# First convolution's projection from rows transposed before their norm's scale is known

## The chip, the cores and the metric

The kernel runs on one core of a Trainium2 chip. The time is that of one execution on the device in microseconds. In the profile PE is the tensor engine (matmuls), PEld its weight loads, DVE the vector engine, ACT the scalar engine, POOL the GpSimd engine and SP the engine that issues the DMA transfers of weights. PEclk is the tensor engine's granted clock as a share of its full speed (1.00 is 2.4 GHz, 0.50 is 1.2 GHz).

## The reference, cut to what matters

Two transformer layers work on 256 rows of 1024 numbers in float32. The change touches the head of the first one: the root-mean-square norm, the projections of the normed rows, and the short causal convolution over the rows that stands behind three of them.

```python
def rmsnorm(x, g):
    y = x * lax.rsqrt(jnp.mean(x * x, axis=-1, keepdims=True) + EPS)
    return y * g

h = rmsnorm(x, norm1_g)
parts = split_cols(h @ w_in)              # q, k, v (512 each), z, beta, alpha (8 each),
                                          # b_q, b_k, b_v, i_q, i_k, i_w, gates
qkv = silu(causal_dwconv(concat([a_q, a_k, a_v]), conv_w))
...
o_a = gated_delta_rule(aq, ak, av, g, beta)
o_b = dsa_attention(bq, bk, bv, iq, ik, iw)
merged = gate_a * (o_a @ w_proj_a) + gate_b * (o_b @ w_proj_b)
x = x + merged @ w_out
x = x + hier_moe(rmsnorm(x, norm2_g), ...)
```

A second layer (a gated recurrence, attention, a feed-forward block) follows; the change doesn't touch it. The norm multiplies each row by one number, its inverse root. A product of the rows with a weight matrix can therefore take that number in before or behind the product, row by row.

## The kernel before, in words

Every large product runs in split precision. An operand is held as a high part (ACT copies it to a rounded float32 type) and a low part (DVE subtracts the high part from it), and each product of 128 columns of the inner dimension is three matmuls: high x high, high x low, low x high. For weights the two parts are `whi` (L298, ACT) and `wlo` (L301, DVE), made from `raw`, which SP's queue loads 512 KB at a time (`wload`, L306); each of the three has a ring of four buffers. For the activations they are the two halves of `hx`, the tiles of an `HT` object: four tiles, each with two blocks of 128 columns.

The normed rows are needed transposed, with the inner dimension on the partitions. A transpose is a matmul of 128 columns of x by a matrix: by the identity it only transposes, by `dg`, the identity times each row's inverse root (L212, DVE), it scales the rows as well. `square` (L217, ACT) sums the squares of half a row at a time, and `row_scale` finds the inverse root from them in some twelve small steps on DVE, then makes `dg`. In the program before, all 16 blocks (two groups of 128 rows, eight blocks each) are scaled transposes (L492), four to a tile of PSUM. DVE multiplies each four by the norm's gain (L495) into `h`, and pairs of blocks are split from there (L254 on ACT, L255 on DVE) into `hT`. The gain, and the weights of the convolution, come from `arow`, whose 56 rows are transposed once (L482) and copied to `ap`.

`hT` feeds, in this order of the program: `zps`, the narrow product for beta and alpha (L543 to L545, 16 columns); `conv(1)`, which makes k, and `conv(0)`, which makes q. `conv` calls `fm`, which multiplies 128 columns of weights at a time with all 256 rows (L373 to L375) in groups of two sums, and for each of the four sums calls `em`: ACT copies the sum from PSUM into `zc` and, scaled, into `cy`; DVE adds the three earlier rows (three L563); ACT takes the tanh; DVE makes the result (L566). Then comes the chain of the delta rule, a generator that `stream` runs up to its mark "v": it takes the softplus of alpha (L386 and behind), works on q and k for each group of rows (DVE, ACT, PE, and four products on POOL, L652 to L657), inverts small triangular blocks with a long row of small DVE steps, and then joins them with products of 64 x 64 (`prod`, L731). Behind it in the program stand `conv(2)` for v, the rest of the chain, and then the projections for the second mixer in four groups (`z_group`: two of 292 columns into `zI`, two of 384 into `zB`), which run in `tm` (L333 to L335), 192 matmuls in all, and the gates (512 columns).

The order on each engine is fixed ahead of the run: a scheduler takes the program and places each instruction by its own estimates of when operands and buffers are there. So a change at the head moves instructions far behind it. PSUM has three tiles for sums (`acc`) and three for the small products of the first stage (`sm`). SP's queue starts with x's first half, the identity (the first 128 columns of the constants `cst`), the two parts of `arow`, x's second half, and then the rest of the constants (L526, 1 MB) ahead of the first weights.

Of the kernel before, what the change touches and what calls it, by code (L numbers as in the profile page):

```python
# [18 lines left out]
S = 256  # L19
# [52 lines left out]
def body(ctx, tc, I, out, dbg=None):  # L72
# [13 lines left out]
    def nm(s):  # L86
        cnt[0] += 1
        return f"{s}{cnt[0]}"
# [74 lines left out]
    SY.dma_start(xt[0][:, 0:512], I["x"][0, 0:128, 0:512])  # L163
    SY.dma_start(xt[0][:, 512:], I["x"][0, 0:128, 512:])
    SY.dma_start(ident, I["cst"][:, 0:128])
    SY.dma_start(arow[48:56], I["norm1_g"][0].rearrange("(r c) -> r c", c=128))
    SY.dma_start(arow[0:48], I["conv_w"][0].rearrange("j (r c) -> (j r) c", c=128))
    SY.dma_start(xt[1], I["x"][0, 128:256, :])
# [306 lines left out]
    dgs = []  # L475
    for t in range(2):
        q = tiny([128, 2])
        for hf in range(2):
            square(xt[t][:, hf * 512:(hf + 1) * 512], q[:, hf:hf + 1])
        dgs.append(row_scale(q)[1])  # L480
# [4 lines left out]
    n1 = ap[:, 48:56]  # L485
    hT = HT(8)
    h32 = [b4([128, 4, S], n="h32") for _ in range(2)]
    for t in range(2):
        for j in range(2):
            ps = sm()  # L490
            for k in range(4):
                T.matmul(ps[:, k * 128:(k + 1) * 128], xt[t][:, (4 * j + k) * 128:(4 * j + k + 1) * 128], dgs[t],  # L492
                         start=True, stop=True)
            y = h32[j][:, :, t * 128:(t + 1) * 128]
            V.tensor_tensor(y, ps.rearrange("p (k t) -> p k t", k=4),  # L495
                            n1[:, 4 * j:4 * j + 4, None].to_broadcast([128, 4, 128]), op=ALU.mult)
            for i in range(2):
                split_psum(y[:, 2 * i:2 * i + 2], *(hT.pair(2 * j + i, q, t * 128, (t + 1) * 128) for q in range(2)))
# [53 lines left out]
    qT, kT, vT = (a4([128, 4, S], n="qkvT") for _ in range(3))  # L552

    def conv(i, dst):
        def em(f, ps):
            zc = sp.tile([128, S + 3], F32, tag="zc", name=nm("zc"), bufs=2)
            G.memset(zc[:, 0:3], 0.0)
            A.activation(zc[:, 3:], ps, AF.Copy)
            y = cv("cy")
            cw = [ap[:, j * 12 + i * 4 + f:j * 12 + i * 4 + f + 1] for j in range(4)]  # L560
            A.activation(y, ps, AF.Copy, scale=cw[3])
            for j in (2, 1, 0):
                V.scalar_tensor_tensor(y, zc[:, j:j + S], cw[j], y, op0=ALU.mult, op1=ALU.add)  # L563
# [1247 lines left out]
```

## Time and profile before

| what | us |
| --- | --- |
| median of three runs | 882.61 |
| lowest and highest of them | 880.13 and 883.9 |
| the profiled execution's own time | 878.45 |
| span of its trace | 876.7 |
| PE busy in the span | 828.0 |
| DVE busy in the span | 599.9 |

The profiled execution is a run of its own, a little faster than the three timed ones. The span runs from the first to the last instruction recorded; the time holds another 1.75 us around it. In the rows further down a matmul's own duration is longer than its pace, since matmuls overlap: the time from one start to the next tells what one costs.

### The profile page before, as it was taken

To read this page: it belongs to the slowest core of one execution; us is meant where nothing else is said; L and a number is where in the kernel's file an instruction comes from. 1 tells how busy PE (TensorE), PEld (TensorE's weight loads), DVE (VectorE), ACT (ScalarE), POOL (GpSimd) and SP (SyncE) were. 2 spreads that over 40 slices of the span, in tenths; PEclk is the share of its full clock that TensorE was granted. 3 is DMA by queue.
4 is the path that set the end of the run, shared out by engine and by line. 5 is a ranking of instruction groups with operands and counts; after the bars stand their busy time and mean duration, and the time that the engine had idled before them with its cause. 6 is when DMAs were issued, how large, how long until landed. Compare 5 with 4: busy or idle time off the path is not lost.

```text
span 876.7 us, 14583 instructions
## 1 busy us (share of the span) xinstructions
PE 828.0 (94%) x5541; PEld 692.7 (79%) x5541; DVE 599.9 (68%) x1301; ACT 418.5 (48%) x742; POOL 59.1 (7%) x74
## 2 busy tenths in 40 slices
PE   5998999999998999998798998999999999999997
PEld 4997878888987665654797985889888888888876
DVE  5977996987677242425769788666886666674564
ACT  5743544566452111114664544665566555663443
POOL 5022030000000000000116002000000000000000
PEclk9999999999998999999899998999999999999999
DMA  8633561345489899965453563255665666665541
GB/s 247 191 87 78 170 194 50 96 148 180 155 324 312 291 397 339 388 202 171 147 149 82 163 208 108 73 170 190 214 197 157 182 190 189 182 211 198 193 157 48
DMA packets 107577, 162.81 MB, mean 186 GB/s; under 512 B 7256, under 2 KB 73312, under 8 KB 107504
## 3 DMA queue, kind: packets, MB, share of 16 engines
q1 hardware_dynamic: 106864, 161.71, 57.9%
q8 instruction: 45, 0.74, 0.3%
q0 software_dynamic: 640, 0.13, 0.2%
q14 instruction: 28, 0.23, 0.1%
HBM read 159.71 MB, written 2.11 MB: 185 GB/s over the span
## 4 chain that ended last, share of the span: by engine, by line
PE 43%; DVE 6%; issue 2%; ACT 1%; POOL 0%; DVEq 0%; POOLq 0%; ACTq 0%
PE acc L368 13%; PE acc L369 6%; PE acc L335 5%; PE acc L334 5%; PE acc L333 5%; PE acc L374 1%; PE acc L375 1%; PE acc L373 1%; PE sm L272 1%; DVE wlo L301 1%; PE sm L1656 1%; PE sm L1560 1%; PE sm L1684 1%; DVE ST L1561 0%; PE sm L1676 0%
## 5 line engine op out<-in xcount | busy, mean ns | idle before, releaser
L301 DVE TENSOR_TENSOR wlo<-raw,whi 128x1024 fp32r<-128x1024 f32 (+4 forms) x203 | 240.0, 1185 | 93.4 <-ACT whi L298 91.6
L298 ACT ACTIVATE whi<-raw 128x1024 fp32r<-128x1024 f32 (+4 forms) x203 | 207.0, 1022 | 147.8 <-PE acc L335 53.4
L368 PE MATMUL acc<-hx,whi 128*128 128x512 f32 x608 | 212.0, 400 | 0.9 <-DVE hx L255 0.9
L369 PE MATMUL acc<-hx,wlo 128*128 128x256 f32 x608 | 160.6, 284 | 0.0
L333 PE MATMUL acc<-whi,hx 128*128 128x512 f32 (+3 forms) x368 | 138.5, 376 | 6.8 <-ACT zI L814 3.7
L334 PE MATMUL acc<-wlo,hx 128*128 128x512 f32 (+3 forms) x368 | 137.2, 373 | 0.1
L335 PE MATMUL acc<-whi,hx 128*128 128x512 f32 (+3 forms) x368 | 137.3, 373 | 0.0
L368 PEld LDWEIGHTS acc<-hx,whi 128*128 128x128 f32 x608 | 109.4, 188 | 22.4 <-DVE hx L255 1.1
L369 PEld LDWEIGHTS acc<-hx,wlo 128*128 128x128 f32 x608 | 114.6, 189 | 8.2 <-issue 1.0
L333 PEld LDWEIGHTS acc<-whi,hx 128*128 128x128 f32 x368 | 69.8, 190 | 18.0 <-ACT zI L814 4.5
L374 PE MATMUL acc<-hx,whi 128*128 128x256 f32 x288 | 82.4, 286 | 1.4 <-DVE hx L258 1.4
L373 PE MATMUL acc<-hx,whi 128*128 128x256 f32 x288 | 81.6, 286 | 1.5 <-ACT hx L257 1.5
L375 PE MATMUL acc<-hx,wlo 128*128 128x256 f32 x288 | 82.7, 288 | 0.0
L335 PEld LDWEIGHTS acc<-whi,hx 128*128 128x128 f32 x368 | 69.8, 190 | 10.0 <-issue 0.2
L334 PEld LDWEIGHTS acc<-wlo,hx 128*128 128x128 f32 x368 | 69.9, 190 | 9.3 <-DVE wlo L301 0.4
L1247 PE MATMUL acc<-we,xg 128*64 128x256 f32 x512 | 64.8, 383 | 0.0
L374 PEld LDWEIGHTS acc<-hx,whi 128*128 128x128 f32 x288 | 55.9, 194 | 2.0 <-DVE hx L258 1.8
L373 PEld LDWEIGHTS acc<-hx,whi 128*128 128x128 f32 x288 | 55.5, 194 | 2.4 <-ACT hx L257 2.0
L375 PEld LDWEIGHTS acc<-hx,wlo 128*128 128x128 f32 x288 | 56.0, 195 | 0.4 <-issue 0.2
L1247 PEld LDWEIGHTS acc<-we,xg 128*64 128x64 f32 x512 | 37.8, 137 | 21.3 <-issue 5.4
L379 ACT ACTIVATE both<-acc 128x256 f32<-128x256 f32 x76 | 28.8, 380 | 33.4 <-PE acc L368 33.4
L380 DVE TENSOR_TENSOR both<-both,acc 128x256 f32<-128x256 f32 x76 | 31.7, 416 | 16.6 <-ACT both L379 15.7
(456 smaller groups left out, 1119.2 us busy)
## 6 DMA issues: line engine op xcount, KB each, us to landing
raw<-in_w_in SPq DMA_DIRECT2D x64, 512.0 KB, 3.7
we<-in_w_exp_gate SPq DMA_DIRECT2D x32, 512.0 KB, 7.6
we<-in_w_exp_up SPq DMA_DIRECT2D x32, 512.0 KB, 8.0
wd<-in_w_exp_down SPq DMA_DIRECT2D x64, 256.0 KB, 6.0
raw<-in_w_ffn_gate SPq DMA_DIRECT2D x22, 512.0 KB, 3.8
raw<-in_w_ffn_up SPq DMA_DIRECT2D x22, 512.0 KB, 3.8
raw<-in_w_ffn_down SPq DMA_DIRECT2D x22, 512.0 KB, 4.3
raw<-in_w_out SPq DMA_DIRECT2D x16, 512.0 KB, 4.4
```

Source lines behind the costliest of these rows:

```text
L298: A.activation(hi[:, :n], raw[:, :n], AF.Copy)
L301: (eng or V).tensor_tensor(lo[:, :n], raw[:, :n], hi[:, :n].bitcast(F32), op=ALU.subtract)
L333: T.matmul(ps[t][:, :n], ht.hi(kk, a, b), wh[:, k], start=kk == 0, stop=False)
L334: T.matmul(ps[t][:, :n], ht.hi(kk, a, b), wl[:, k], start=False, stop=False)
L335: T.matmul(ps[t][:, :n], ht.lo(kk, a, b), wh[:, k], start=False, stop=kk == K - 1)
L368: two = [lambda: T.matmul(ps[f], wh[:, k, c], ht.both(kk), start=kk == 0, stop=kk == K - 1), lambda: T.matmul(ps[f][:, :S], wl[:, k, c], h ...
L369: lambda: T.matmul(ps[f][:, :S], wl[:, k, c], ht.hi(kk), start=False, stop=False)]
L373: T.matmul(ps[f][:, :S], wh[:, k, c], ht.hi(kk), start=kk == 0, stop=False)
L374: T.matmul(ps[f][:, :S], wh[:, k, c], ht.lo(kk), start=False, stop=False)
L375: T.matmul(ps[f][:, :S], wl[:, k, c], ht.hi(kk), start=False, stop=kk == K - 1)
L380: V.tensor_tensor(both, both, ps[f][:, :S], op=ALU.add)
L1247: T.matmul(ph[64 * q:64 * q + 64, i * 256:(i + 1) * 256], xgs[pr // 2][k // 4][:, k % 4, e * 64:(e + 1) * 64], ups[ex][k // 4, i][:, k % 4 ...
```

## The change

x's four quarters now go first on SP's queue, and the identity and `arow` go to ACT's queue. `arow` is transposed first. Then all 16 blocks are transposed by the identity alone (L270), as soon as x is there, and each block is split on its own with the gain as the scale (`transpose_in` with `gk`: L257 on ACT, L258 on DVE, 128 columns each) into a first `HT`, `rT`. The squares stand behind that, with all the steps of the inverse roots. Two matmuls of a matrix of ones with `dg` (L494) spread the inverse roots of all rows over the 128 partitions, and ACT copies them to `rrow`. `conv(1)` runs on `rT`, and its `em` takes each sum from PSUM by a product with `rrow` on DVE (L510) in place of ACT's copy; ACT then makes `cy` from that. Behind `conv(1)` the 16 blocks are made once more, scaled (L272), and split block by block (L257, L258) into `hT`, which `conv(0)` and everything behind it use. `zps` comes after that. The load of the constants' rest now stands behind four weight loads on SP's queue.

```diff
--- before.py
+++ after.py
@@ -160,12 +160,12 @@
 
     xt = [b4([128, D], n="x") for _ in range(2)]
     arow = sp.tile([56, 128], F32, tag="t128", name=nm("arow"), bufs=4)
-    SY.dma_start(xt[0][:, 0:512], I["x"][0, 0:128, 0:512])
-    SY.dma_start(xt[0][:, 512:], I["x"][0, 0:128, 512:])
-    SY.dma_start(ident, I["cst"][:, 0:128])
-    SY.dma_start(arow[48:56], I["norm1_g"][0].rearrange("(r c) -> r c", c=128))
-    SY.dma_start(arow[0:48], I["conv_w"][0].rearrange("j (r c) -> (j r) c", c=128))
-    SY.dma_start(xt[1], I["x"][0, 128:256, :])
+    A.dma_start(ident, I["cst"][:, 0:128])
+    for t in range(2):
+        for hf in range(2):
+            SY.dma_start(xt[t][:, hf * 512:(hf + 1) * 512], I["x"][0, t * 128:(t + 1) * 128, hf * 512:(hf + 1) * 512])
+    A.dma_start(arow[48:56], I["norm1_g"][0].rearrange("(r c) -> r c", c=128))
+    A.dma_start(arow[0:48], I["conv_w"][0].rearrange("j (r c) -> (j r) c", c=128))
 
 
     def rsqrt(v, shape):
@@ -472,30 +472,53 @@
 
 
     w_in = I["w_in"][0]
-    dgs = []
-    for t in range(2):
-        q = tiny([128, 2])
-        for hf in range(2):
-            square(xt[t][:, hf * 512:(hf + 1) * 512], q[:, hf:hf + 1])
-        dgs.append(row_scale(q)[1])
     gps = sm()
     T.transpose(gps[:, 0:56], arow, ident[0:56, 0:56])
     ap = cpool.tile([128, 56], F32, name="ap")
     V.tensor_copy(ap, gps[:, 0:56])
     n1 = ap[:, 48:56]
+
+    rT = HT(8)
+    for j in range(2):
+        for t in range(2):
+            transpose_in({t: xt[t]}, ht=rT, ts=(t,), js=(j,), gk=n1)
+    qs_ = [tiny([128, 2]) for _ in range(2)]
+    for t in range(2):
+        for hf in range(2):
+            square(xt[t][:, hf * 512:(hf + 1) * 512], qs_[t][:, hf:hf + 1])
+    ones_ = sp.tile([128, 128], F32, tag="t128", name=nm("one"), bufs=4)
+    V.memset(ones_, 1.0)
+    dgs = [row_scale(q)[1] for q in qs_]
+    rps = sm()
+    for t in range(2):
+        T.matmul(rps[:, t * 128:(t + 1) * 128], ones_, dgs[t], start=True, stop=True)
+    rrow = b1([128, S], n="rr")
+    A.activation(rrow, rps[:, 0:S], AF.Copy)
+
+    qT, kT, vT = (a4([128, 4, S], n="qkvT") for _ in range(3))
+
+    def conv(i, dst, ht, scale=None):
+        def em(f, ps):
+            zc = sp.tile([128, S + 3], F32, tag="zc", name=nm("zc"), bufs=2)
+            G.memset(zc[:, 0:3], 0.0)
+            y = cv("cy")
+            cw = [ap[:, j * 12 + i * 4 + f:j * 12 + i * 4 + f + 1] for j in range(4)]
+            if scale is None:
+                A.activation(zc[:, 3:], ps, AF.Copy)
+                A.activation(y, ps, AF.Copy, scale=cw[3])
+            else:
+                V.tensor_tensor(zc[:, 3:], ps, scale, op=ALU.mult)
+                A.activation(y, zc[:, 3:], AF.Copy, scale=cw[3])
+            for j in (2, 1, 0):
+                V.scalar_tensor_tensor(y, zc[:, j:j + S], cw[j], y, op0=ALU.mult, op1=ALU.add)
+            th = cv("ct")
+            A.activation(th, y, AF.Tanh, scale=0.5)
+            V.scalar_tensor_tensor(dst[:, f], th, 1.0, y, op0=ALU.add, op1=ALU.mult)
+        fm(ht, w_in, i * 512, 4, em)
+    conv(1, kT, rT, rrow)
     hT = HT(8)
-    h32 = [b4([128, 4, S], n="h32") for _ in range(2)]
     for t in range(2):
-        for j in range(2):
-            ps = sm()
-            for k in range(4):
-                T.matmul(ps[:, k * 128:(k + 1) * 128], xt[t][:, (4 * j + k) * 128:(4 * j + k + 1) * 128], dgs[t],
-                         start=True, stop=True)
-            y = h32[j][:, :, t * 128:(t + 1) * 128]
-            V.tensor_tensor(y, ps.rearrange("p (k t) -> p k t", k=4),
-                            n1[:, 4 * j:4 * j + 4, None].to_broadcast([128, 4, 128]), op=ALU.mult)
-            for i in range(2):
-                split_psum(y[:, 2 * i:2 * i + 2], *(hT.pair(2 * j + i, q, t * 128, (t + 1) * 128) for q in range(2)))
+        transpose_in({t: xt[t]}, ht=hT, dg={t: dgs[t]}, ts=(t,), gk=n1)
 
     prow = cpool.tile([44, 128], F32, name="prow")
     G.dma_start(prow[0:16], I["b_gate"][0].rearrange("(r c) -> r c", c=128))
@@ -549,24 +572,7 @@
         T.transpose(zp2[:, t * 16:(t + 1) * 16], zbT[:, t * 128:(t + 1) * 128], ident[0:16, 0:16])
     V.tensor_copy(zb, zp2[:, 0:32].rearrange("p (t c) -> p t c", t=2))
 
-    qT, kT, vT = (a4([128, 4, S], n="qkvT") for _ in range(3))
-
-    def conv(i, dst):
-        def em(f, ps):
-            zc = sp.tile([128, S + 3], F32, tag="zc", name=nm("zc"), bufs=2)
-            G.memset(zc[:, 0:3], 0.0)
-            A.activation(zc[:, 3:], ps, AF.Copy)
-            y = cv("cy")
-            cw = [ap[:, j * 12 + i * 4 + f:j * 12 + i * 4 + f + 1] for j in range(4)]
-            A.activation(y, ps, AF.Copy, scale=cw[3])
-            for j in (2, 1, 0):
-                V.scalar_tensor_tensor(y, zc[:, j:j + S], cw[j], y, op0=ALU.mult, op1=ALU.add)
-            th = cv("ct")
-            A.activation(th, y, AF.Tanh, scale=0.5)
-            V.scalar_tensor_tensor(dst[:, f], th, 1.0, y, op0=ALU.add, op1=ALU.mult)
-        fm(hT, w_in, i * 512, 4, em)
-    conv(1, kT)
-    conv(0, qT)
+    conv(0, qT, hT)
 
     def hv(ap):
 
@@ -803,7 +809,7 @@
 
     dl_ = delta()
     stream("a", dl_)
-    conv(2, vT)
+    conv(2, vT, hT)
     stream("a", dl_)
 
     zB = [b4([128, 768], n="zB") for _ in range(2)]
```

The order of PE at the head, before: `sm` are PSUM tiles of small products, `x_74` and `x_75` the two groups of rows, `dg` the scales, `hx` the split blocks, `acc` the sums of 128 columns.

```order
L482 MATMUL sm_127<-cst,arow_76 128x56
L492 MATMUL sm_137<-dg_103,x_74 128x128 x4
L492 MATMUL sm_147<-dg_103,x_74 128x128 x4
L492 MATMUL sm_157<-dg_125,x_75 128x128 x4
L492 MATMUL sm_167<-dg_125,x_75 128x128 x4
L528 MATMUL sm_203<-cst,prow 128x44
L543 MATMUL acc_213<-hx_131,whi_216 16x256
L373 MATMUL acc_252<-hx_131,whi_256 128x256
L373 MATMUL acc_253<-hx_131,whi_256 128x256
```

After, the first nine:

```order
L476 MATMUL sm_84<-cst,arow_76 128x56
L270 MATMUL sm_92<-cst,x_74 128x128 x4
L270 MATMUL sm_105<-cst,x_75 128x128 x4
L270 MATMUL sm_118<-cst,x_74 128x128 x4
L270 MATMUL sm_131<-cst,x_75 128x128 x4
L373 MATMUL acc_198<-hx_88,whi_202 128x256
L374 MATMUL acc_198<-hx_88,whi_202 128x256
L373 MATMUL acc_199<-hx_88,whi_202 128x256
L374 MATMUL acc_199<-hx_88,whi_202 128x256
```

The scaled transposes ahead of the first sum (L492) have become unscaled ones (L270); `zps` (L543) is gone from the head, and the first sum is worked on with nothing between. In the order after, the scaled transposes stand behind the whole of `conv(1)` (`acc_283` is `conv(1)`'s last sum, `acc_494` and `acc_495` are `conv(0)`'s first, `acc_458` is `zps`):

```order
L375 MATMUL acc_283<-hx_91,wlo_318 128x256
L272 MATMUL sm_370<-dg_171,x_74 128x128 x4
L272 MATMUL sm_383<-dg_171,x_74 128x128 x4
L272 MATMUL sm_396<-dg_188,x_75 128x128 x4
L566 MATMUL acc_458<-hx_366,whi_461 16x256
L373 MATMUL acc_494<-hx_366,whi_498 128x256
L373 MATMUL acc_495<-hx_366,whi_498 128x256
L567 MATMUL acc_458<-hx_366,whi_461 16x256
L568 MATMUL acc_458<-hx_366,wlo_463 16x256
L374 MATMUL acc_494<-hx_366,whi_498 128x256
```

Three of the four groups stand there in a row; the last (`sm_409`) follows twelve matmuls of `conv(0)` and `zps` later. On DVE in the same place, before, in `conv(1)`'s sums (`cy`, `ct` and `zc` are the tiles of `em`, `qkvT` its result, `t` the softplus):

```order
L301 TENSOR_TENSOR wlo_456<-raw_452,whi_454 128x1024
L566 SCALAR_TENSOR_TENSOR qkvT_250<-ct_322,cy_317 128x256
L563 SCALAR_TENSOR_TENSOR cy_328<-zc_325,ap,cy_328 128x256
L390 TENSOR_SCALAR t_603<-t_601 128x16
L563 SCALAR_TENSOR_TENSOR cy_328<-zc_325,ap,cy_328 128x256
L392 RECIPROCAL t_605<-t_603 128x16
L563 SCALAR_TENSOR_TENSOR cy_328<-zc_325,ap,cy_328 128x256
L301 TENSOR_TENSOR wlo_510<-raw_506,whi_508 128x1024
L566 SCALAR_TENSOR_TENSOR qkvT_250<-ct_333,cy_328 128x256
L563 SCALAR_TENSOR_TENSOR cy_401<-zc_398,ap,cy_401 128x256
```

And after:

```order
L301 TENSOR_TENSOR wlo_584<-raw_580,whi_582 128x1024
L513 SCALAR_TENSOR_TENSOR cy_273<-zc_271,ap,cy_273 128x256
L258 SCALAR_TENSOR_TENSOR hx_366<-sm_370,ap,hx_366 128x128
L510 TENSOR_TENSOR zc_355<-acc_283,rr_193 128x256
L516 SCALAR_TENSOR_TENSOR qkvT_196<-ct_279,cy_273 128x256
L513 SCALAR_TENSOR_TENSOR cy_346<-zc_344,ap,cy_346 128x256
L258 SCALAR_TENSOR_TENSOR hx_366<-sm_370,ap,hx_366 128x128
L513 SCALAR_TENSOR_TENSOR cy_346<-zc_344,ap,cy_346 128x256
L258 SCALAR_TENSOR_TENSOR hx_366<-sm_396,ap,hx_366 128x128
L513 SCALAR_TENSOR_TENSOR cy_346<-zc_344,ap,cy_346 128x256
L258 SCALAR_TENSOR_TENSOR hx_367<-sm_370,ap,hx_367 128x128
```

The softplus steps have gone behind, and the products with `rrow` (`rr_193`, L510) and the second set of splits (L258 into `hx_366` and on) have come in between `conv(1)`'s sums. The third place is PE around the first triangular product of the chain. Before, in the last of the four groups of `z_group` (`acc_1700`; `acc_2190` is the first sum of the gates):

```order
L333 MATMUL acc_1700<-whi_1757,hx_134 128x384
L334 MATMUL acc_1700<-wlo_1759,hx_134 128x384
L335 MATMUL acc_1700<-whi_1757,hx_134 128x384
L333 MATMUL acc_1700<-whi_1757,hx_134 128x384
L731 MATMUL sm_924<-DD_905,LT_632 64x64 x16
L334 MATMUL acc_1700<-wlo_1759,hx_134 128x384
L335 MATMUL acc_1700<-whi_1757,hx_134 128x384
L333 MATMUL acc_2190<-whi_2194,hx_131 128x512
L334 MATMUL acc_2190<-wlo_2196,hx_131 128x512
L335 MATMUL acc_2190<-whi_2194,hx_131 128x512
L731 MATMUL sm_943<-DT_906,X_941 64x64 x16
```

And after, where `acc_1773` and `acc_1774` are the sums of the last group for the two groups of rows:

```order
L335 MATMUL acc_1698<-whi_1755,hx_369 128x384
L333 MATMUL acc_1773<-whi_1777,hx_366 128x384
L334 MATMUL acc_1773<-wlo_1779,hx_366 128x384
L335 MATMUL acc_1773<-whi_1777,hx_366 128x384
L333 MATMUL acc_1773<-whi_1777,hx_366 128x384
L334 MATMUL acc_1773<-wlo_1779,hx_366 128x384
L335 MATMUL acc_1773<-whi_1777,hx_366 128x384
L737 MATMUL sm_998<-DD_979,LT_706 64x64 x16
L333 MATMUL acc_1774<-whi_1777,hx_366 128x384
```

Of the 192 matmuls of the four groups, 190 stand ahead of the first triangular product (L731) before, and 150 ahead of the same product (L737) after; the others follow it. `conv(2)` stands whole ahead of the second row half's products (L665 before, L671 after) in the order after.

## Rows read from the trace of the kernel before

**Rows 1.** The page's first part: busy us, share of the span, instructions.

```profile
PE 828.0 (94%) x5541; PEld 692.7 (79%) x5541; DVE 599.9 (68%) x1301; ACT 418.5 (48%) x742; POOL 59.1 (7%) x74
```

**Rows 2.** Stretches: length; busy of PE, PEld, DVE, ACT, POOL; PEclk; DMA share; GB/s.

```profile
24.00:48.00 24.00, 23.77 (x197) 23.34 (x197) 23.56 (x65) 16.35 (x33) 0.80 (x8) 1.00 0.62 173
48.00:104.00 56.00, 50.46 (x404) 47.04 (x403) 45.70 (x128) 22.54 (x41) 11.77 (x10) 0.97 0.38 113
0.00:104.00 104.00, 87.83 (x692) 82.49 (x693) 84.18 (x237) 51.84 (x100) 24.31 (x44) 0.98 0.55 158
105.90:130.00 24.10, 23.07 (x410) 19.40 (x410) 23.28 (x44) 12.31 (x19) 6.41 (x8) 1.00 0.64 194
130.00:220.00 90.00, 90.00 (x679) 75.27 (x678) 72.84 (x194) 53.51 (x119) 2.56 (x3) 1.00 0.40 120
```

**Rows 3.** Timeline of the start: start, length, engine, instruction, [idle before, what ended it].

```profile
3.50 0.63 ACT L217 ACTIVATE junk<-x 128x512 f32<-128x512 f32 x1 [1.47 <-DMA x<-in_x]
...
4.26 0.63 ACT L217 ACTIVATE junk<-x 128x512 f32<-128x512 f32 x1
...
5.58 0.32 PE L482 MATMUL sm<-cst,arow 56*128 56x56 f32 x1 [5.58 <-DMA arow<-in_conv_w]
...
13.18 1.04 ACT L298 ACTIVATE whi<-raw 128x1024 fp32r<-128x1024 f32 x1
...
13.52 2.05 PE L492 MATMUL sm<-dg,x 128*128 128x128 f32 x16 [1.73 <-DVE hx L255]
...
15.91 0.29 PE L543 MATMUL acc<-hx,whi 128*16 128x256 f32 x1 [0.15 <-ACT hx L254]
```

**Rows 4.** Timeline of PE in a convolution and in a 384-column projection.

```profile
20.93 0.28 PE L374 MATMUL acc<-hx,whi 128*128 128x256 f32 x1
21.05 0.28 PE L375 MATMUL acc<-hx,wlo 128*128 128x256 f32 x1
...
97.46 0.33 PE L333 MATMUL acc<-whi,hx 128*128 128x384 f32 x1
97.64 0.33 PE L334 MATMUL acc<-wlo,hx 128*128 128x384 f32 x1
```

**Rows 5.** Timeline near 424 us, where another norm is split block by block.

```profile
424.59 0.62 ACT L257 ACTIVATE hx<-sm,par 128x128 fp32r<-128x128 f32 x2 [0.42 <-DVE hx L258]
...
424.99 0.61 DVE L258 SCALAR_TENSOR_TENSOR hx<-sm,par,hx 128x128 fp32r<-128x128 f32 x2
```

**Rows 6.** Timeline of DVE at the start and in the convolutions.

```profile
11.83 0.69 DVE L495 TENSOR_TENSOR h<-sm,ap 128x512 f32<-128x512 f32 x1
...
13.03 1.09 DVE L255 TENSOR_TENSOR hx<-h,hx 128x256 fp32r<-128x256 f32 x3
...
29.78 1.22 DVE L301 TENSOR_TENSOR wlo<-raw,whi 128x1024 fp32r<-128x1024 f32 x1
30.91 0.42 DVE L566 SCALAR_TENSOR_TENSOR qkvT<-ct,cy 128x256 f32<-128x256 f32 x1
31.25 0.48 DVE L563 SCALAR_TENSOR_TENSOR cy<-zc,ap,cy 128x256 f32<-128x256 f32 x1
31.64 0.17 DVE L394 TENSOR_TENSOR t<-t,t 128x16 f32<-128x16 f32 x1
```

**Rows 7.** Timeline of the delta chain: GpSimd's second row half, the first triangular product.

```profile
75.00 1.90 POOL L652 TENSOR_TENSOR dl<-t,cst 128x512 f32<-128x512 f32 x1 [11.19 <-DVE t L648]
...
105.91 0.80 PE L731 MATMUL sm<-DD,LT 64*64 64x64 f32 x20
```

**Rows 8.** PE's longest wait behind 48 us, and two stretches with their PEclk.

```profile
85.23 0.44 PE L333 MATMUL acc<-whi,hx 128*128 128x384 f32 x1 [3.24 <-ACT zI L814]
...
86.40:89.60 3.20, 3.20 (x12) 3.20 (x11) 3.06 (x11) 0.00 (x0) 0.00 (x0) 0.50 0.70 157
96.80:101.00 4.20, 4.18 (x24) 4.12 (x24) 4.13 (x13) 0.70 (x1) 0.00 (x0) 1.00 0.98 344
```

## What the change was predicted to do

> **What bounds the kernel now.** I read the page's busy shares first: the tensor engine (PE) has work for 94% of the span, the vector engine (DVE) for 68% [rows 1]. Shares are averages, so next the stretches [rows 2]. From 130 to 220 us PE is busy for all 90 us: whatever it owes when it comes there is paid in full. From 24 to 48 us both engines are full (PE 23.8, DVE 23.6 of 24), so that a longer DVE queue holds up PE. From 48 to 104 us PE works 50.5 and DVE 45.7 of 56: here the chain of the delta rule passes back and forth between DVE, GpSimd and PE. The edit works on the first 48 us, and its price is read in two places: when PE has finished `conv(0)`, and how much independent matmul work is left for PE when the chain's first triangular product (L731, at 105.91 [rows 7]) may run. Behind 220 us the two programs' PE orders are the same again but for small exchanges, so a lead or a lag is handed on.
>
> **The start.** PE's unbroken run begins at 15.91 [rows 3], after the squares, the inverse root, the scaled transposes and their splits. In the changed program the raw transposes need no root. ScalarE (ACT) sets their pace: its first square still begins at 3.50, since x's first half lands as before; L482 and its copy, which give the norm's gain column, come some 0.5 earlier than at 5.58, so the first split can run at about 5.7. Ahead of the first weight copy ACT then has 11 split copies (two take 0.62 [rows 5], so 0.31 each) and three more squares (3.50 to 4.26, so 0.76 each [rows 3]): 3.4 + 2.3 = 5.7, to 11.4; with that copy (1.04 [rows 3]) the first matmul of `conv(1)` stands at 12.5: **3.4 us earlier**. The wait for the first low half of the weights behind it (one L301) I count as in the program before.
>
> **Work added to PE.** The 16 raw transposes lie in time in which PE has nothing to do. The scaled ones don't any more: before, they ran ahead of 15.91; now they stand between `conv(1)` and `conv(0)`, 16 matmuls in two passes each. The second half of them took 2.05 us for 16 passes [rows 3], so **+4.1 us**; the two matmuls that spread the scale are four passes, +0.5.
>
> **Work added to DVE.** Removed: four L495 (0.69 long, about 0.6 of the queue) and eight L255 (three in 1.09, so 0.36) [rows 6]: 2.4 + 2.9 = 5.3. Added: 32 split subtractions of 128 columns (two in 0.61, so about 0.28 in a run [rows 5]) = 9.0, and four products of a PSUM sum with the scale row. No row shows that product; the nearest are L566 (0.34 from one to the next) and L563 (0.39) [rows 6], so 1.4 to 1.6; by the PSUM read of L495 taken at half its width it would be 1.2. Sum: **+5.2 us**, in the stretch in which DVE is full.
>
> **The stall between the convolutions.** PE ends `conv(1)` at 12.5 + 0.75 (first wait) + 96 x 0.12 [rows 4] + 0.5 = 25.3 and the first three groups of scaled transposes at 28.4. Then it needs the second set of splits. They stand in DVE's queue among the work on `conv(1)`'s sums. That queue gets there late: up to the first sum it holds 16 subtractions (4.5), some two dozen steps of the two roots (0.15 each, 3.6), four L301 (1.13 each, 4.5) and the scale diagonals (0.6), 13.2 us from 5.4 on, plus some 1.5 of waiting for ACT, so 20.1 to 20.4. From there to the last split: 4 products 1.4, 12 L563 4.7, 4 L566 1.4, 3 L301 3.4, 16 subtractions 4.6, small ones 0.6: 16.1, and some 0.7 of waiting: 37.3. PE has only the narrow product for beta and alpha, 18 matmuls of `conv(0)` and the last scaled group to fill 28.4 to 37.3: 42 x 0.12 + 1.0 + 0.3 = 6.3. **Stall: 2.6 us**; 0 if DVE had no waits at all and PE came late, 4 if ACT's alternation with DVE costs full turns (0.40 from copy to subtraction in both directions [rows 5]). At the end of `conv(0)` PE therefore lies -3.4 + 4.1 + 0.5 + 2.6 = **+3.8 us** behind.
>
> **The delta chain.** The order shows the second price. Before, 190 of the 192 matmuls of the index and attention projections stand ahead of the first L731; now 150 do. The 40 are 384 columns wide, 0.175 each [rows 4]: **7.0 us** of PE work not yet done when the chain's products start. When is that? DVE was busy 84.2 of the first 104 us [rows 2]. Now +5.2, less the four weight halves that now stand behind it (768 columns each, three quarters of 1.13: -3.4): 86.0. Its idle time before was 19.8. Of this 5.4 at the start remain; I find 4 to 5 of small waits to the end of `conv(0)`, and twice 3 to 4.5 in which it waits for GpSimd's four products (first at 75.00 in the second half row [rows 7]), since the softplus steps no longer lie under the convolution and there is less to fill with: 18.5 in all, so 104.5 where 104 was. L731 then moves by +0.5, and 7.0 + 0.5 less the 1.0 us that PE waits in 105.9 to 130 now (24.1 - 23.1 [rows 2]), which owed work can fill, is **+6.5 us**.
>
> The two counts, +3.8 if nothing further is lost and +6.5 by the order, bound the forecast; I take the middle, **+5.2 us**. The profiled execution took 878.45 us (span 876.70 and 1.75 around it), which becomes 883.7. The runs shown have a median of 882.61, 4.2 above it; on that scale: **887.8 us**. Its own range is 885 to 890.
>
> The DMA edits cost nothing: the identity and the gain rows leave x's queue, and the rest of the constants goes behind four weight tiles; two copies of L1034/L1035 and the narrow weights' copy on ACT then wait for it, ahead of the last split copy. That split is needed by PE at about 18.3, and I put the landing there too; a microsecond later would show as a microsecond of PE wait.
>
> **Rivals.**
> A, DVE's waits go (not slower). DVE has 10.3 us idle from 48 to 104 [rows 2]; if the added 5.2 us fill them and the chain reaches L731 at 100.9, then -5 + 7.0 - 1.0 = +1.0: 883.6. It decides if GpSimd's products of the second half row start before 75.00 [rows 7]. For it: the idle time is there. Against: it is time in which DVE waits for this very chain.
> B, PE's waits go (faster). From 48 to 104 us PE is idle for 5.5 us [rows 2], 3.24 of them at one evacuation (85.23), behind which it runs at half the granted clock from 86.4 to 89.6, 1.6 us lost [rows 8]. With no stall between the convolutions (+1.2) and all of this gone (-7.1): -5.9, 876.7. It needs PE late and the chain not late.
> C, the clock falls (slower still). At 86.40 to 89.60 the granted clock is 0.50 (1.2 GHz) after 3.24 us without a matmul, against 1.00 (2.4 GHz) at 96.8 to 101 [rows 8]. The changed program has PE nearly idle from about 8.5 to 12.5, and the gap at 28.4. Each such fall costs the 1.6 us of that row: +5.2 + 3.2 = +8.4, 891.0. The Trainium skill (TensorE: Matmul & The Clock Gate, Part 4: PE-mode transpose) says that transposes in that mode don't count as work for the clock gate. By that rule the raw transposes would not raise the clock, and the fall at the start would be certain; no run here shows it.
> D, the early start fails: if the gain column or the identity lands late on ACT's queue, or ACT is slower than summed, PE starts at 15.9 as before: +5.2 + 3.4 = +8.6, 891.2.
>
> **How the numbers follow.** Forecast 0.38, A 0.27, B 0.13, C 0.15, D 0.07. A has gained by the order: that 40 matmuls fewer are planned ahead of the chain's first product can also mean that the chain comes early. A measurement of this kernel can tell 0.5%, here 4.4 us, from no change. Slower by more: two thirds of the forecast (0.25), C and D nearly whole (0.21), a little of A: 0.48. Within: a third of the forecast, most of A, a little of B: 0.41. Faster by more: most of B, 0.11. The range leaves out B and the far end of C and D: 880.5 to 892.5.
>
> **What would show it.** Right: the first L373 near 12.5; four groups of L272 between the convolutions; a PE wait of 2 to 4 us for splits (L257 or L258) near 28 to 37; `conv(0)` ending near 46.5 where it was near 42.5; DVE full from 20 to 52; L737 (L731 before) at 105 to 107 with most of a projection group left. Wrong: `conv(0)` ending before 43.5, or the chain's products at about 100. A granted clock below 1.00 in the first 16 us or near 30 would be C; a first L373 past 15, D.

## The result, and the profile after

The changed kernel takes **891.31 us** (median of 4 runs, 890.41 to 892.62) where the kernel before takes 881.37 (4 runs of the same comparison, 878.6 to 883.9): a ratio of **1.0125** (95% interval 1.01 to 1.0149), 9.9 us slower by the medians. The profiled execution took 891.79 us, with a span of 890.0; against the profiled execution of before that is 13.3 us. The forecast was 887.8, and 5.2 us more than before, with 885 to 890 as its own range. Two kernels further down have executions in two groups, and their profiles are of the longer one: `e4_scaled_first` took 880.6 to 883.8 us in seven of ten and 886.5 to 887.2 in three, `v1_no_scaled_set` 880.3 to 882.7 in seven and 890.7 to 893.3 in three.

The page's first part, and the stretches that answer to [rows 1] and [rows 2] (the columns are those of [rows 2]):

```profile
PE 837.1 (94%) x5561; PEld 700.0 (79%) x5561; DVE 603.5 (68%) x1326; ACT 423.1 (48%) x761; POOL 60.6 (7%) x74
```
```profile
24.00:48.00 24.00, 20.87 (x166) 18.85 (x166) 21.43 (x54) 15.48 (x39) 0.51 (x5) 1.00 0.43 123
48.00:104.00 56.00, 49.32 (x408) 45.41 (x407) 44.41 (x142) 22.94 (x42) 10.57 (x13) 0.94 0.34 95
0.00:104.00 104.00, 84.91 (x654) 77.85 (x655) 78.72 (x242) 52.50 (x114) 22.87 (x44) 0.97 0.49 137
130.00:220.00 90.00, 88.47 (x683) 72.59 (x682) 74.86 (x195) 50.71 (x111) 9.77 (x9) 1.00 0.43 124
```

PE is busy 9.1 us longer in the whole and idle 4.2 us longer. The stretch from 24 to 48, which was full on both engines, now has 3.1 us without PE and 2.6 without DVE. DVE, which the prediction saw as the engine that would be full, was busy *less* in the first 104 us (78.7 against 84.2).

The start and the place between the convolutions, in the timeline of PE after:

```profile
13.30 0.58 PE L373 MATMUL acc<-hx,whi 128*128 128x256 f32 x1
...
13.90 0.41 PE L373 MATMUL acc<-hx,whi 128*128 128x256 f32 x1
14.11 0.41 PE L374 MATMUL acc<-hx,whi 128*128 128x256 f32 x1
...
18.57 0.28 PE L375 MATMUL acc<-hx,wlo 128*128 128x256 f32 x1
18.69 0.28 PE L373 MATMUL acc<-hx,whi 128*128 128x256 f32 x1
...
28.02 2.84 PE L272 MATMUL sm<-dg,x 128*128 128x128 f32 x24
32.34 0.29 PE L566 MATMUL acc<-hx,whi 128*16 128x256 f32 x1 [1.49 <-ACT hx L257]
33.34 0.29 PE L567 MATMUL acc<-hx,whi 128*16 128x256 f32 x1 [0.48 <-DVE hx L258]
...
35.54 1.16 PE L272 MATMUL sm<-dg,x 128*128 128x128 f32 x8 [0.91 <-DVE hx L258]
...
50.92 0.49 PE L608 MATMUL sm<-cst,qkvT 128*128 128x128 f32 x3
...
112.91 0.59 PE L737 MATMUL sm<-DD,LT 64*64 64x64 f32 x6
```

The first matmul comes at 13.30, 2.6 us earlier than the 15.91 of [rows 3]. Up to 18.4 us the starts lie 0.21 apart, behind that 0.12 as in [rows 4]. Then come the scaled transposes, three waits for the second set of splits, and L608, the first transpose of the delta chain, which stands right behind the last matmul of `conv(0)` here and in the program before. There it ran at 42.91, here at 50.92: **8.0 us later**.

```profile
42.91 0.27 PE L602 MATMUL sm<-cst,qkvT 128*128 128x128 f32 x1
```

The chain's first triangular product runs at 112.91, 7.0 later than the 105.91 of [rows 7].

Behind that, PE waits twice for a low half of weights. The first two rows are PE's waits from 60 to 106 and from 106 to 112 us (total, times, longest); then the copy of the first one's high half on ACT, DVE's timeline ahead of it, and two stretches:

```profile
PE acc L334 <- DVE wlo L301: 2.9, 1, 2.9
PE acc L334 <- DVE wlo L301: 2.0, 1, 2.0
```
```profile
83.65 0.69 ACT L298 ACTIVATE whi<-raw 128x584 fp32r<-128x584 f32 x1 [3.93 <-PE acc L335]
```
```profile
85.22 0.42 DVE L673 TENSOR_TENSOR LT<-sm,dl 128x256 f32<-128x256 f32 x1 [1.17 <-POOL dl L662]
86.47 0.42 DVE L674 TENSOR_TENSOR QK<-sm,di 128x256 f32<-128x256 f32 x1 [0.82 <-POOL di L663]
...
89.75 0.77 DVE L301 TENSOR_TENSOR wlo<-raw,whi 128x584 fp32r<-128x584 f32 x1
```
```profile
90.20:97.00 6.80, 5.92 (x23) 5.57 (x24) 4.68 (x14) 1.26 (x2) 0.00 (x0) 0.50 0.41 116
110.70:114.10 3.40, 3.09 (x27) 2.65 (x29) 2.66 (x5) 1.88 (x6) 0.00 (x0) 0.50 0.59 169
```

The weights' high half was ready at 84.3, but its low half stands in DVE's order behind the steps of the chain that wait for GpSimd. PE stops at 87.7, and the granted clock is 0.50 (1.2 GHz) for 6.8 us there and 3.4 us at the second wait, where before it was 0.50 for one stretch of 3.2 us [rows 8]. The last mark is the first L368, with which the two mixers' gates begin (what the order lists call gates, the 512 columns of `tm`, is z and stands ahead of it). PE reaches it at 157.88 before and at 172.05 after:

```profile
157.88 0.50 PE L368 MATMUL acc<-hx,whi 128*128 128x512 f32 x1
```
```profile
172.05 0.39 PE L368 MATMUL acc<-hx,whi 128*128 128x512 f32 x1
```

That is 14.2 us later, so the whole of the 13.3 us between the two profiles is made by then.

### The profile page after: what moved, and what is told of

The parts are those of the page before. It is cut to its first block, busy times and chain, and to the rows that moved or that the text cites. A ratio compares the mean times of both kernels' runs of the same rounds, so it can differ in the third digit from the quotient of the medians.

```text
span 890.0 us, 14674 instructions
## 1 busy us (share of the span) xinstructions
PE 837.1 (94%) x5561; PEld 700.0 (79%) x5561; DVE 603.5 (68%) x1326; ACT 423.1 (48%) x761; POOL 60.6 (7%) x74
## 4 chain that ended last, share of the span: by engine, by line
PE 43%; DVE 5%; issue 2%; ACT 1%; POOL 0%; DVEq 0%; POOLq 0%; ACTq 0%
PE acc L368 13%; PE acc L369 6%; PE acc L335 5%; PE acc L334 5%; PE acc L333 5%; PE acc L374 1%; PE acc L375 1%; PE acc L373 1%; PE sm L272 1%; PE sm L1566 1%; DVE wlo L301 1%; PE sm L1662 1%; PE sm L1690 1%; PE sm L1682 0%; DVE W L1561 0%
## 5 line engine op out<-in xcount | busy, mean ns | idle before, releaser
L368 PE MATMUL acc<-hx,whi 128*128 128x512 f32 x608 | 212.9, 400 | 1.6 <-DVE hx L255 0.9
L368 PEld LDWEIGHTS acc<-hx,whi 128*128 128x128 f32 x608 | 109.7, 188 | 23.7 <-DVE hx L255 1.1
L373 PE MATMUL acc<-hx,whi 128*128 128x256 f32 x288 | 82.0, 289 | 1.5 <-ACT hx L257 1.5
L333 PEld LDWEIGHTS acc<-whi,hx 128*128 128x128 f32 x368 | 70.6, 192 | 15.8 <-ACT zI L820 3.1
L335 PEld LDWEIGHTS acc<-whi,hx 128*128 128x128 f32 x368 | 70.9, 193 | 10.5 <-issue 0.6
L373 PEld LDWEIGHTS acc<-hx,whi 128*128 128x128 f32 x288 | 55.5, 195 | 2.8 <-ACT hx L257 2.0
L380 DVE TENSOR_TENSOR both<-both,acc 128x256 f32<-128x256 f32 x76 | 31.7, 417 | 19.4 <-ACT both L379 18.4
```

Source lines behind the costliest of these rows:

```text
L333: T.matmul(ps[t][:, :n], ht.hi(kk, a, b), wh[:, k], start=kk == 0, stop=False)
L335: T.matmul(ps[t][:, :n], ht.lo(kk, a, b), wh[:, k], start=False, stop=kk == K - 1)
L368: two = [lambda: T.matmul(ps[f], wh[:, k, c], ht.both(kk), start=kk == 0, stop=kk == K - 1), lambda: T.matmul(ps[f][:, :S], wl[:, k, c], h ...
L373: T.matmul(ps[f][:, :S], wh[:, k, c], ht.hi(kk), start=kk == 0, stop=False)
L380: V.tensor_tensor(both, both, ps[f][:, :S], op=ALU.add)
```

## The experiments

All ratios are against the kernel before, run on the same chip beside each kernel; its medians there were 879.3 to 880.6 us. "The end of `conv(0)`" is the start of the chain's first transpose, as above.

**The transfers.** `d1_dma_only` is the program before with the first hunk of the diff alone; `d2_old_dma` is the changed program with that hunk undone.

> The program before with the DMA edit alone: x's quarters first on SP's queue, identity and gain rows on ACT's queue; the rest of the constants stays ahead of the weights. Theory H (the loss sits in PE's first 50 us: a slow start, the second set of transposes, and a stall for their splits): nothing of that is here, so 879 to 883. Rival D (the new order of transfers is what costs): 886 or more, with the first convolution's matmuls later than 15.9.

> The changed program with the old order of the first transfers (identity and gain rows on SP's queue, x's second half in one piece); the rest of the constants still behind the weights. Theory H: the same as the changed program to 2 us, 889 to 893; the first L373 moves by less than 1 us from 13.30. Rival D: 885 or less.

Measured: 881.79 us, 1.0013 (0.9988 to 1.0038), and 890.87 us, 1.012 (1.0098 to 1.0143). The order of the transfers is not where the 9.9 us went. Two parts of the expectations were missed. `d1_dma_only` has a slow start of its own: its `conv(0)` ends at 45.87, 3.0 us later than before, while its time rose by 1.1 us (up to 3.3 by the interval). And with the *old* order the changed program's first L373 ran at 10.78, not 13.30. Its first weight copy stands behind five split copies on ACT, with the new order behind ten, and ACT took the second square at 4.16, before the gain column was there:

```profile
4.16 0.63 ACT L217 ACTIVATE junk<-x 128x512 f32<-128x512 f32 x1
...
7.07 0.37 ACT L257 ACTIVATE hx<-sm,ap 128x128 fp32r<-128x128 f32 x1 [2.19 <-PE sm L270]
...
9.66 1.06 ACT L298 ACTIVATE whi<-raw 128x1024 fp32r<-128x1024 f32 x1
```

Of these 2.5 us, 1.2 were left at the end of `conv(0)` (49.74) and 0.5 of span at the end.

**The stall.** `e4_scaled_first` moves the second set ahead of `conv(1)` in the program; the work is the same.

```diff
+    hT = HT(8)
+    for t in range(2):
+        transpose_in({t: xt[t]}, ht=hT, dg={t: dgs[t]}, ts=(t,), gk=n1)
     conv(1, kT, rT, rrow)
-    hT = HT(8)
-    for t in range(2):
-        transpose_in({t: xt[t]}, ht=hT, dg={t: dgs[t]}, ts=(t,), gk=n1)
```

> The changed program with the 16 scaled transposes and their splits written ahead of conv(1) instead of behind it, so that PE makes them among conv(1)'s matmuls and the splits lie under these. Same work on every engine. Theory H: PE no longer waits between the convolutions (4.4 us in the changed program), conv(0) ends near 46.5 instead of 50.9, and the time falls by 3 to 5 us to 886 to 888. Rival V (the added DVE work as such is what costs, wherever it stands): the same DVE work, so 890 or more; a conv(0) that ends early while the time stays would mean that the lead is lost again in the delta chain.

Measured: 882.98 us, **1.004** (1.0021 to 1.0059). That is some 7 us less than the changed program, more than expected, with the same work on every engine. The list of PE's waits from 13 to 48 us is empty, and PE is busy throughout:

```profile
16.00:45.10 29.10, 29.10 (x244) 28.25 (x243) 27.29 (x71) 19.89 (x48) 0.51 (x5) 1.00 0.63 169
```
```profile
45.14 0.71 PE L608 MATMUL sm<-cst,qkvT 128*128 128x128 f32 x5
```

`conv(0)` ends at 45.14, 5.8 earlier. The two waits for low halves are gone as well: from 48 to 172 us PE waits for evacuations (5.8 us in all, the longest 3.6) and for steps of the chain (2.0 us in all, 1.0 of it at the first triangular product). So the place of the second set, and the order that follows from it further on, is about two thirds of the loss by the two ratios. DVE's added work as such (rival V) is not: it is all in this run too.

**PE's slow start.** `e6_warm` puts ten matmuls that nobody reads into PE's idle stretch.

```diff
+    wps = acc()
+    for k in range(10):
+        T.matmul(wps[:, 0:128], xt[1][:, 896:1024], ident, start=True, stop=True)
     qs_ = [tiny([128, 2]) for _ in range(2)]
```

> The changed program with ten more matmuls of 128 columns (20 passes) that nobody reads, on PE between its third and fourth group of unscaled transposes, where it stands idle from 8.8 to 12.3 us. Theory C (PE's slow first matmuls, 0.21 us apart instead of 0.12 until 18.4 us, come from that idle stretch): the first matmuls of conv(1) are 0.12 apart, conv(1) ends 1.5 to 2 us earlier, and the time falls by 1 to 2 us to 889 to 890. Rival: the pace is set by something else (weights or splits not there), and stays 0.21; or the stall behind conv(1) grows by what is won, and the time stays at 891.

Measured: 892.24 us, 1.0134 (1.0109 to 1.0159). Theory C's mechanism is shown: with PE at work up to 11.2 us, the first matmuls are 0.12 apart from the second on.

```profile
8.29 2.88 PE L487 MATMUL acc<-cst,x 128*128 128x128 f32 x20
...
12.94 0.39 PE L373 MATMUL acc<-hx,whi 128*128 128x256 f32 x1 [0.36 <-ACT whi L298]
13.16 0.28 PE L374 MATMUL acc<-hx,whi 128*128 128x256 f32 x1
13.28 0.29 PE L373 MATMUL acc<-hx,whi 128*128 128x256 f32 x1
```

`conv(1)` ends 2.1 us earlier (25.93 against 28.02). But nothing of it is left in the time. Of the 2.1 us, 1.1 reach the end of `conv(0)` (49.84), and the second set's last split comes 1.1 us earlier as well. The changed program's first, then this run's:

```profile
40.05 0.35 DVE L258 SCALAR_TENSOR_TENSOR hx<-sm,ap,hx 128x128 fp32r<-128x128 f32 x1
```
```profile
38.92 0.35 DVE L258 SCALAR_TENSOR_TENSOR hx<-sm,ap,hx 128x128 fp32r<-128x128 f32 x1
```

`conv(0)` ends 10.9 us behind that split in both, and in `d2_old_dma` too (38.88 and 49.74). So its end follows the splits, and PE's start and pace count only as far as they bring these forward. Here the granted clock is 0.50 from 33.2 to 36.6 besides; the two waits for low halves come again, 2.9 and 1.9 us long, and the second stretch at 0.50 is 6.8 us, not 3.4.

**PE's work alone.** `e5_extra_pe` adds 16 scaled transposes between the convolutions to the program *before*, written to PSUM and read by nobody.

> The program before with 16 scaled transposes more between the convolutions, 32 passes on PE whose result nobody reads; nothing added on DVE or ACT. Theory H (PE's work up to the end of conv(0) is paid in full): conv(0) ends 3.8 us later than 42.9 (32 x 0.12) and the time rises by 3 to 5 us, to 883 to 885. Rival I (PE's 5.5 idle us from 48 to 104 take it up): conv(0) ends later, but the time stays within 1.5 us of the program before.

Measured: 882.07 us beside a base of 879.31, **1.0039** (1.0017 to 1.0062), so 3.4 us (1.5 to 5.5). `conv(0)` ended at 47.38, 4.5 us later and not 3.8, and the transposes took 3.7:

```profile
32.28 3.73 PE L573 MATMUL sm<-dg,x 128*128 128x128 f32 x32
```

So PE's work ahead of the chain is paid, nearly in full by the middle of the interval. It is also about what is left in `e4_scaled_first`, which suggests, but doesn't show, that the rest of the loss is this work.

**The waits for low halves.** `e7_wlo_pool` makes the two low halves on GpSimd (`held` hands an engine to the weight splits that follow).

```diff
+    held += [(None, None, V)] * 5 + [(None, None, G)] + [(None, None, V)] * 4 + [(None, None, G)]
     z_group(zI, 2832, 0, 292)
```

> The changed program with the low halves of two weight tiles made on GpSimd instead of DVE: the last tile of zI's second group and the first of zB's second, the two for which PE waits 2.9 and 2.0 us at 90.6 and 111.0 in the changed program, because they stand in DVE's order behind steps of the delta chain. Theory W (these two waits, with the half-clock stretches behind them, are the second half of the loss): the waits shrink to under 1 us each, less of 90 to 115 us is at the granted clock 0.50, and the time falls by 3 to 6 us to 885 to 888. Rival: PE then waits for the chain instead, and the time stays at 890 or more.

Measured: 888.61 us, 1.0091 (1.0063 to 1.0119): some 3 us less, though the interval overlaps that of the changed program; the median lies between what the theory and its rival expected. PE's waits from 60 to 112 us:

```profile
PE acc L334 <- DVE wlo L301: 4.0, 1, 4.0
...
PE acc L334 <- POOL wlo L301: 0.2, 1, 0.2
```

The wait of 2.9 is gone. The one of 2.0 moved to the next tile of the same group, whose low half is still on DVE behind the chain, and grew to 4.0. The theory holds for the first wait; the second shows that PE comes to the chain too early or the chain too late there, whichever tile is next.

**Without the second set.** In `v1_no_scaled_set` all projections run on `rT`. The convolutions, the narrow product and the gates take the row of scales behind the sum, the projections with rows on partitions take a scale in ACT's copy, and z's scale goes into a later factor. `v3_no_scaled_old_dma` is the same with the old order of transfers.

```diff
-    hT = HT(8)
-    for t in range(2):
-        transpose_in({t: xt[t]}, ht=hT, dg={t: dgs[t]}, ts=(t,), gk=n1)
...
-    A.activation(zbT, zps[0:16, :S], AF.Copy)
+    V.tensor_tensor(zbT, zps[0:16, :S], rrow[0:16], op=ALU.mult)
...
-    conv(0, qT, hT)
+    conv(0, qT, rT, rrow)
...
-            A.activation(z[t][:, a:b], ps, AF.Copy)
-        tm(hT, w_in, c0 + a, b - a, em)
+            A.activation(z[t][:, a:b], ps, AF.Copy, scale=ry[t][:, 0:1])
+        tm(rT, w_in, c0 + a, b - a, em)
...
+                        V.tensor_tensor(ps, ps, scale, op=ALU.mult)
                     A.activation(sg[hf][:, f], ps, AF.Tanh, bias=bb, scale=0.5)
```

> The changed program without the second, scaled set: all projections of the first layer's norm run on the unscaled split, and the row scale is multiplied in behind each (a row of scales for the convolutions, the narrow product and the gates on DVE, a scale per partition in ACT's copies for the other projections). On PE 32 passes fewer, on DVE 16 split subtractions fewer, eight products with the row of scales more for the convolutions and 16 for the gates. Theory H: no stall and no second set, so conv(0) ends near 41.5 (13.3 + 1.9 slow start + 216 matmuls at 0.12 + 0.4) against 42.9 before, and the time is 877 to 882, at or a little under the program before. Rival V (DVE's added products cost): 884 or more.

> The same without the scaled set, with the old order of the first transfers, under which the changed program's first L373 came at 10.8 instead of 13.3. Theory H: conv(0) ends near 40, 1.5 us earlier than with the new order, and the time is 875 to 880. Rival: the lead of the start is lost again by the delta chain, whose steps and waits set the time from there, and the time is that of the run with the new order.

Measured: 882.17 us, 1.0054 (1.0013 to 1.0095), and 880.68 us, 1.0009 (0.9983 to 1.0034). Both medians lie just above the range that was expected. In the second, `conv(0)` ends at 42.78, as before, not at 40, and the chain's first product comes later than before, with PE waiting for it:

```profile
111.93 1.33 PE L743 MATMUL sm<-DD,LT 64*64 64x64 f32 x20 [3.93 <-ACT DD L730]
```

PE waits for the chain there and not the chain for PE; the rival of that expectation, that the lead is lost to the chain, fits what happened. Whether the new order of transfers costs the difference between the two is open: their intervals overlap, as do those of the other two pairs.

**The softplus.** The chain begins with the softplus of alpha, which needs the narrow product. DVE's last step of the softplus (L403) ran at 47.83 before, at 60.69 in the changed program, at 56.56 in `e4_scaled_first` and at 58.44 in `v3_no_scaled_old_dma`, since the narrow product has moved behind `conv(1)`. Three runs move it ahead again, on the unscaled split with the row of scales behind it.

> The run with the scaled set written ahead of conv(1), and besides the narrow product for beta and alpha moved ahead of conv(1), on the unscaled split with the row scale multiplied in behind. The softplus of alpha then lies under the convolutions again. Theory S (with the stall gone, the chain is held by the softplus, which ends at 56.6 there and at 47.8 in the program before): it ends near 48, the last product of q and k in the second row half runs near 76 instead of 81.4, and the time falls by 1.5 to 4 us to 879 to 881. Rival: DVE's amount of work holds the chain, whatever comes first; the last product of q and k stays within 1.5 us of 81 and the time near 883.

> The changed program with that one move alone: the narrow product ahead of conv(1) on the unscaled split, the scaled set still between the convolutions. Theory: the narrow product's 24 matmuls no longer lie in the stall behind conv(1), so PE waits there up to 2.8 us longer (7 instead of 4.4), conv(0) ends near 51 as before, but the softplus ends at 50 or earlier instead of 60.7, and the time is 887 to 890. Rival: the lateness of the softplus costs nothing in the changed program, since PE comes as late: 890 to 893.

> The run without the scaled set and with the old order of transfers, with the narrow product moved ahead of conv(1) besides. Theory S: the softplus ends near 48 instead of 58.4, the first triangular product of the chain runs at 107 or earlier instead of 111.9, PE's wait of 3.9 us there shrinks, and the time is 875 to 879, under the program before. Rival (DVE's added products hold the chain): 879.5 to 882, no better than without the move.

Measured: `e8_zb_first` 886.93 us, 1.0082 (1.0047 to 1.0116); `e9_zb_first_only` 888.54 us, 1.0104 (1.008 to 1.0128); `v5_zb_first` **877.02 us, 0.996** (0.9937 to 0.9983). Theory S falls in the first: the softplus ended 4.2 us earlier (52.34, not the 48 expected), but the last product of q and k in the second row half ran at 86.8, later than the 81.4 of `e4_scaled_first`, which neither theory nor rival had, and the time did not fall: its median is 4 us higher, with intervals that overlap. Now PE waits within `conv(0)` for room in PSUM, and `conv(0)` ends at 49.95. PE's waits from 16 to 60 us:

```profile
PE acc L373 <- ACT cy L508: 3.8, 3, 2.8
```

L508 evacuates a sum of `conv(0)`; that the splits and products now crowd ACT and DVE at this other place is a reading of that wait, and no run tests it. In the second, the time is as expected, but its interval overlaps that of the changed program; the softplus came at 55.3, not at 50, and PE's waits behind `conv(1)` did not grow (2.6 us on the list, against 2.9). The third beats both kernels. Its softplus ends at 53.39, its first triangular product runs at 111.77 and not at 107: the expected step did not happen, so the gain over `v3_no_scaled_old_dma` is measured (the intervals only touch) and its cause is open.

**Who sets the time then.** `v6_zb_first_warm` is `v5_zb_first` with the ten idle-time matmuls.

> The fastest run so far (no scaled set, old order of transfers, narrow product first) with the ten matmuls that nobody reads on PE ahead of its first products, as in the earlier run with them. Theory B (up to 112 us the delta chain on DVE sets the time in this version, PE waiting 3.3 us for it at 111.8): the 0.21 pace ends earlier, conv(0) ends up to 1 us earlier, PE waits that much longer at the first triangular product, and the time is that of the run without them to 1.5 us (875.5 to 878.5). Rival (PE still sets the time): 1 to 2 us less.

Measured: 877.69 us, 0.9965 (0.9944 to 0.9987), no change. `conv(0)` ends 0.7 us earlier (42.62 against 43.35), and PE waits for the chain as before, 3.2 us where it was 3.3:

```profile
111.03 1.20 PE L746 MATMUL sm<-DD,LT 64*64 64x64 f32 x32 [3.18 <-ACT DD L733]
```

The chain's product moved with `conv(0)`'s end (0.7 us), which theory B had not expected; in the span it is 0.9 us, too little for the runs to tell.

## Why the prediction came out as it did

The time lay inside the range and on the forecast's side, but the loss was nearly twice the forecast. The forecast's own range ended at 890, and the outer range reached further only for rivals C and D; that the time fell inside is in part luck. The terms, in the prediction's own order:

- **The start, -3.4: measured -2.6.** The transpose for the gain column came no earlier (L476 at 5.79), and the first split waited until all four transposes of its tile were done, 1.1 us that the sum left out; it ran at 7.19, not at 5.7.
- **PE's pace at the start: taken at 0.12, measured 0.21 up to 18.4 us, +1.9.** This was the first half of rival C, but for its mark: no granted clock below 1.00 showed in the page, and the pace did. The fall that C had at 28 did not come (the starts are 0.12 apart from 33.5 on), so its 891.0 was met by other terms. The Trainium skill (TensorE: Matmul & The Clock Gate, Part 4: PE-mode transpose) says that transposes in that mode don't count as work for the clock. By that rule the unscaled transposes from 6.0 to 8.9 us could not help; the trace agrees in so far as they didn't. Ten plain matmuls in the idle 3.4 us behind them did help; whether the kind of work or that idle stretch kept the pace low, no run tells.
- **The second set on PE, +4.1 and +0.5: measured 4.0 (2.84 + 1.16) and 0.4.** Right, and `e5_extra_pe` shows that such work is paid.
- **The stall, +2.6: measured some 4, the upper bound that was named.** 2.9 us of it are the three waits in PE's rows above; the rest are shorter gaps. The last subtraction ran at 40.05 where 37.3 was worked out. DVE was not full on the way, as the sum took it to be: it waited 2.5 us for the row of scales. That row waited for the second L494, which stands on PE at 22.28, though its diagonal was made at 20.12:

```profile
20.12 0.28 DVE L212 TENSOR_SCALAR dg<-cst,ry 128x128 f32<-128x128 f32 x1
```
```profile
22.28 0.39 PE L494 MATMUL sm<-dg,one 128*128 128x128 f32 x2
```
```profile
23.12 0.76 DVE L510 TENSOR_TENSOR zc<-acc,rr 128x256 f32<-128x256 f32 x2 [2.51 <-ACT rr L496]
```

- **Sum at the end of `conv(0)`: +3.8 forecast, +8.0 measured.** -2.6 + 1.9 + 4.0 + 0.4 + 4 make 7.7; 0.3 are small gaps. The sum adds up along PE, but what set this end was the splits: in `e6_warm` and `d2_old_dma` PE began sooner or ran faster, and `conv(0)` gained what the last split gained. Of the 4.2 us between forecast and measurement, 2.8 are the later last split; the other 1.4 are matmuls and gaps behind it.
- **The chain's first product: +0.5 forecast, +7.0 measured.** This is the step that failed. It was worked out from DVE's amount of work: 86.0 us and 18.5 idle. In the first 104 us DVE did 78.7 and stood idle for 25.3, because the chain starts from `conv(0)`'s results and moved with them. From the end of `conv(0)` to the product it is 62.0 us, 63.0 before. This distance is no constant: it is 60.4 to 63.0 in seven of the programs here, but 65.0 to 69.2 in the other seven (`e4`, `e8`, `e9` and the four `v` runs), where PE waits 1.0 to 3.9 us for the chain at the product. What holds the chain in those is open.
- **The 40 matmuls ahead of it, +7.0: right in kind, by another way.** That PE has less independent work done there showed as +14.2 us at the first L368. Of these, 8.0 came from the head. In the stretch behind, PE is idle for 10.1 us where it was 6.8, and the half-clock stretches (10.2 us against 3.2) cost an estimated 3.5 more: together the remaining 6.2, within 0.7. The prediction noted the four weight halves behind the chain on DVE, but only as work that DVE is rid of. Who would wait for them was not asked.
- **Product with the scale row, 1.4 to 1.6 for four:** 0.33 from one start to the next (28.53 to 28.86), so 1.3, a little under.
- **Rivals.** A and B did not happen. D did not (the first L373 came at 13.30), though the start lost 0.8 us of its lead.

What stays open is how much of the loss between 60 and 172 us belongs to each of the two waits, whether the last third of the loss is PE's added work alone, and why the profiled pair differs by 13.3 us where the medians differ by 9.9. A part of the second is that the profiled execution of before was 3 us faster than its median.

## What to carry to other kernels

Work that is made twice so that a first product can start early must be placed where its second making lies under other work: here the same instructions cost 1.25% behind the first product and 0.4% among it. When an edit moves a chain against a stream of independent work, ask for each low half, copy or load that the scheduler puts behind the chain who will wait for it. And a few microseconds' lead at the head is worth what the first engine that limits behind it lets through: three times here (`d2_old_dma`, `e6_warm`, `v6_zb_first_warm`) a lead of 0.7 to 2.5 us was made at the head, and none of it could be told from noise in the time.

## What the runs showed of the hardware

The granted clock of a profile can read 1.00 where the engine, by the spacing of its starts, ran at its lower level. The changed program's profile reads 1.00 from 13.3 to 18.4 us, with starts 0.21 us apart for 256 columns. The profile of `e7_wlo_pool`, whose edit lies further back and whose starts there are as far apart, reads 0.50 at the same place:

```profile
12.30:19.00 6.70, 6.52 (x28) 5.92 (x29) 6.70 (x24) 5.70 (x12) 2.34 (x3) 0.50 0.87 169
```

In the program before, PE had worked for 2.05 us right ahead of its first product and began at 0.12; in `d1_dma_only`, the same program begun 1 us later behind waits of 1.3 and 1.2 us, the clock was 0.50 from 16.1 to 22.9:

```profile
16.10:22.90 6.80, 6.08 (x29) 4.34 (x30) 5.17 (x13) 1.98 (x7) 0.00 (x0) 0.50 0.66 154
```

And the same subtraction on GpSimd was about twice as long as on DVE: the low half of 768 columns took 1.85 us there (one instruction, in `e7_wlo_pool`), on DVE 0.92 to 0.95.
